# A gated three-branch decoder layer on one core: products moved into two gaps, branch weights told sooner, and work tied behind the ends of projection halves

## The chip, the cores and the metric

The kernel runs on one core of a Trainium2 chip. Its measure is the device time of one execution in microseconds (us), as the median of several runs on the chip. The program is written with a tile framework: Python code issues instructions to the engines, and a scheduler in the framework settles in which order they stand on each engine, within the dependences, by an estimate of its own. A tie (`tc.issue_after(ins)`) asks that what is issued inside it stands behind a given instruction.

## What is computed

One layer over 1024 tokens of width 1024 (cut to what matters here):

```
h = rms_norm(x); parts of h @ w_in go to three branches and their gates
A: sparse attention, 8 heads of 64: an indexer picks 256 keys for each query
B: latent attention, 8 heads, query and key from low-rank projections
M: 4 heads over 256 fixed memory tokens
each branch: (o * silu(z)) @ w_branch, then * sigmoid(gate); the sum @ w_out + x
```

All products run in float32 precision built from two parts: a matrix is split in a high part (suffix h, an FP32R cast on ACT) and a low part (suffix l, the rest, a subtraction on DVE or POOL), and each product is three matmuls, h*h, h*l and l*h (`mm3`, lines 281 to 284).

## The kernel before

**Stages.** In order of time: keys and values of the memory (products `mkps` and `mvps`), the normed and transposed `x` (kept whole as `hTh`, `hTl`), the query of M and its attention, the low-rank projections, attention B from 285 to 511 us, the indexer, branch M (its silu products `z`, `y`, projection `br`) around 690 to 790 us, branch B around 790 to 915 us, the query/key/value projections of A (`qkv(p)` for four pairs of heads: p = 0 runs in the middle of branch M, 1 in the middle of branch B, 2 and 3 behind them), attention A up to about 1220 us, branch A, and the output projection.

**PE's fillers.** The sigmoid gates of all branches are 512-wide products `f` that depend on `hTh` alone. In an attention a `Filler` (lines 360 to 398) hands out such products in steps of one `mm3`: `fill.run(n)` at a place lets n steps out. `PREB` holds four such counts for the start of attention B: at the loading of the first keys, ahead of `k_prep(0, 0)`, ahead of the first `q_prep`, and behind it (lines 560 to 567). `k_prep` transposes the keys `xk` (tile `bkt`), which POOL and DVE have scaled (lines 980 to 983) with a factor that POOL raises to a power (line 238).

**Weights.** `wload` (line 250) issues a DMA into a raw tile, casts it on ACT (line 245) and subtracts on DVE (line 248). Raw tiles have two buffers here (`pool_raw[:] = [2, 8, 768]`), split branch weights seven of 512 columns (`wkind`). Tiles of a kind are handed out in turn, so a load waits until the buffer's last user is done, and what stands behind it in the issuing engine's queue waits too. In `branch` (line 1331) the products go block by block, d = 0 to 7, each in halves j = 0, 1 of 12 matmuls; weights are told up to three blocks, gate values `tg` up to three buffers and attention outputs `osb` two buffers ahead. A half ends in a multiplication on DVE, `ab` for M (line 1400) and `am` for B (line 1408), which frees the PSUM bank, and in a store from POOL's queue.

**The half's remainder.** `qkv(p)` makes 8 tiles of 24 matmuls of 384 columns; each half of four ends in norms and rope on DVE, a power on POOL, and a closure `scaled` (lines 1459 to 1467): the scaling of q on POOL (`a_xq`) and k on DVE (`a_xk`), a cast and subtraction (`a_qs`) and two stores. It is kept in `behind` and run by `catch_up` later: behind the second tile of the next half, ahead of `ab` or `am`, or behind a `z` in `early`. In the tiles' names the pair's half stands first: `a_1xk` is the second half's.

**Background work.** The selection of the 256 keys runs in small steps on ACT and DVE beside all this (names that begin with k, and `idx`).

## Time and profile before

| what | value |
|---|---|
| time, median of 3 runs | 1387.42 us (1385.16 to 1388.04) |
| the profiled execution's own time, and its span | 1386.62 us, 1384.8 us |
| mean granted clock of TensorE, as a share of full speed | 0.995 |
| PE busy, matmuls | 1348.4 us, 97% of the span, 7408 |
| DVE, ACT, POOL busy | 1004.3 us (73%), 708.9 us (51%), 235.0 us (17%) |

Busy time is the time in which an engine had an instruction in work; PE's is drawn from start to modelled end, so consecutive matmuls overlap, and the pace is read from the distance of starts. An idle time carries in brackets the instruction that ended it. Line numbers are those of the kernel before; the changed kernel's lie 7 to 28 lines further down.

### The profile page before, as it was taken

How to read it: one execution, taken by the hardware profiler on the slowest of the kernel's cores; microseconds unless marked ns; L12 is line 12 of the kernel's file. 1: busy time of each engine (PE TensorE's matmuls, PEld its weight loads, DVE VectorE, ACT ScalarE, POOL GpSimd, SP SyncE). 2: the span in 40 equal slices, each digit the busy share in tenths (PEclk: the TensorE clock that was granted, in tenths of full speed). 3: DMA queues.
4: the chain of work that ended last, by engine and by line, in shares of the span. 5: the costliest groups of instructions: out<-in, count | busy, mean ns of one | idle time of the engine just before them, and what ended most of it. 6: DMA issues, size and time to landing. Idle time of an engine off the chain costs nothing. (4 is left out here: it accounts for less than half of the span.)

```text
span 1384.8 us, 20968 instructions
## 1 busy us (share of the span) xinstructions
PE 1348.4 (97%) x7408; PEld 1161.1 (84%) x7408; DVE 1004.3 (73%) x2417; ACT 708.9 (51%) x1546; POOL 235.0 (17%) x271
## 2 busy tenths in 40 slices
PE   8999999999999999999999999999899999999998
PEld 6998888878888888977798889779888888887787
DVE  5945445678888884298787788678858888867883
ACT  6635443256666662164665656543336665653440
POOL 2141002611110101100004201422240000002422
PEclk9999999999999999999999999999999999999999
DMA  7411222231111117310332841792643514218677
GB/s 265 128 47 54 79 63 61 97 88 54 58 43 43 50 32 268 121 54 24 118 103 88 293 108 45 194 208 82 166 154 95 152 55 114 69 61 268 212 202 177
DMA packets 160265, 159.00 MB, mean 115 GB/s; under 512 B 38688, under 2 KB 115488, under 8 KB 160160
## 3 DMA queue, kind: packets, MB, share of 16 engines
q1 hardware_dynamic: 147952, 126.72, 30.4%
q0 software_dynamic: 10592, 28.84, 7.7%
q10 hardware_dynamic: 1616, 2.10, 0.4%
q8 instruction: 58, 0.95, 0.3%
q14 instruction: 47, 0.39, 0.1%
HBM read 106.77 MB, written 50.86 MB: 114 GB/s over the span
## 5 line engine op out<-in xcount | busy, mean ns | idle before, releaser
L1080 ACT ACTIVATE kag<-idx,kaT 128x896 bf16<-128x896 f32 (+2 forms) x96 | 83.2, 866 | 43.5 <-DVE kaT L1101 34.2
L1074 DVE TENSOR_SCALAR_CACHE_REDUCE kdj<-idx,kdT 128x1024 bf16<-128x1024 f32 (+2 forms) x96 | 92.5, 964 | 1.1
L282 PE MATMUL f<-hTh,f_0h 128*128 128x512 f32 x184 | 79.0, 430 | 1.6 <-ACT fo L382 0.9
L282 PE MATMUL f<-hTh,f_1h 128*128 128x512 f32 x184 | 76.1, 414 | 0.0
L283 PE MATMUL f<-hTl,f_1h 128*128 128x512 f32 x184 | 74.2, 403 | 0.0
L284 PE MATMUL f<-hTh,f_1l 128*128 128x512 f32 x184 | 73.9, 402 | 0.0
L284 PE MATMUL f<-hTh,f_0l 128*128 128x512 f32 x184 | 73.8, 401 | 0.0
L283 PE MATMUL f<-hTl,f_0h 128*128 128x512 f32 x184 | 73.5, 399 | 0.0
L1671 POOL TENSOR_TENSOR ac<-ac,tg 128x512 f32<-128x512 f32 x16 | 25.5, 1602 | 253.4 <-DVE tg L1670 250.7
L382 ACT ACTIVATE fo<-f 128x512 f32<-128x512 f32 x48 | 28.8, 601 | 39.7 <-PE f L284 35.9
L1274 ACT ACTIVATE irl<-is 128x512 f32<-128x512 f32 (+1 forms) x80 | 37.7, 527 | 15.4 <-DVE idx L1280 12.6
L282 PEld LDWEIGHTS f<-hTh,f_0h 128*128 128x128 f32 x184 | 35.1, 191 | 8.2 <-ACT fo L382 2.4
L1280 DVE SCALAR_TENSOR_TENSOR idx<-irl,wi,idx 128x1024 f32<-128x1024 f32 (+5 forms) x42 | 39.8, 948 | 1.9 <-ACT irl L1274 0.3
L284 PEld LDWEIGHTS f<-hTh,f_0l 128*128 128x128 f32 x184 | 34.9, 190 | 6.8
L284 PEld LDWEIGHTS f<-hTh,f_1l 128*128 128x128 f32 x184 | 34.7, 188 | 6.0
L283 PEld LDWEIGHTS f<-hTl,f_1h 128*128 128x128 f32 x184 | 34.8, 189 | 4.3
L283 PEld LDWEIGHTS f<-hTl,f_0h 128*128 128x128 f32 x184 | 35.1, 191 | 3.6
L282 PEld LDWEIGHTS f<-hTh,f_1h 128*128 128x128 f32 x184 | 34.7, 189 | 4.1
L1272 PE MATMUL is<-kih,iqT 128*128 128x512 f32 (+1 forms) x80 | 29.7, 376 | 2.3 <-ACT irl L1274 2.1
L237 POOL TENSOR_SCALAR kf<-kss 128x8 f32<-128x8 f32 x8 | 2.3, 285 | 151.7 <-DVE kss L972 146.3
L1273 PE MATMUL is<-kil,iqT 128*128 128x512 f32 (+1 forms) x80 | 27.4, 354 | 0.0
L1317 DVE SCALAR_TENSOR_TENSOR sz<-sz,z 128x512 f32<-128x512 f32 x24 | 16.4, 685 | 14.5 <-ACT sz L1316 14.4
(1331 smaller groups left out, 4825.1 us busy)
## 6 DMA issues: line engine op xcount, KB each, us to landing
s_tg<-fo SPq DMA_DIRECT2D x48, 256.0 KB, 2.0
tg<-s_tg SPq DMA_DIRECT2D x48, 256.0 KB, 4.5
f_0r<-in_w_in_dram SPq DMA_DIRECT2D x23, 256.0 KB, 3.0
f_1r<-in_w_in_dram SPq DMA_DIRECT2D x23, 256.0 KB, 3.0
xx<-in_x_dram SPq DMA_DIRECT2D x8, 512.0 KB, 8.5
tb<-in_w_out_dram SPq DMA_DIRECT2D x16, 256.0 KB, 5.8
s_t<-tb POOLq DMA_DIRECT2D x16, 256.0 KB, 4.7
osb<-s_o SPq DMA_DIRECT2D x16, 256.0 KB, 3.2
```

The source lines that it names most:

```text
L282: nc.tensor.matmul(ps, ah, bh, start=start, stop=False)
L283: nc.tensor.matmul(ps, ah, bl, start=False, stop=False)
L284: nc.tensor.matmul(ps, al, bh, start=False, stop=stop)
L382: nc.scalar.activation(o, ps, AF.Tanh, scale=0.5)
L1074: nc.vector.tensor_scalar(out=junk, in0=idx[t], scalar1=T[:, i:i + 1], scalar2=0.0, op0=ALU.is_ge, op1=ALU.add, accum_out=cnt[:, i:i + 1])
L1080: nc.scalar.activation(junk, idx[t], AF.Sign, bias=T[:, i:i + 1], accum_out=cnt[:, i:i + 1])
L1272: nc.tensor.matmul(sp[:, 0:w], q_, kih[:, k0:k0 + w], start=True, stop=False)
L1273: nc.tensor.matmul(sp[:, 0:w], q_, kil[:, k0:k0 + w], start=False, stop=True)
L1274: nc.scalar.activation(rl[:, k0:k0 + m], sp[:, 0:m], AF.Relu)
L1280: i_ = nc.vector.scalar_tensor_tensor(out=acc[:, 0:n], in0=rl[:, 0:n], scalar=wc, in1=acc[:, 0:n], op0=ALU.mult, op1=ALU.add)
L1317: zi[0] = nc.vector.scalar_tensor_tensor(out=sz, in0=sz, scalar=1.0, in1=pz[j], op0=ALU.add, op1=ALU.mult)
L1671: nc.gpsimd.tensor_tensor(ac, ac, tg, op=ALU.add)
```

## The change

It does six things. (1) The 16 transposes that PE does before its first data come go into one PSUM tile, and 14 more such transposes are tied behind those of the memory's third column block. (2) `PREB` goes from (0, 0, 0, 16) to (0, 12, 0, 7), and `k_prep(0, 0)` is tied behind the last matmul so issued. (3) Weights of branches M and B are told four blocks ahead, with eight buffers; `osb` shares one ring of four buffers with `tg` there. (4) `catch_up` comes behind `ab` or `am` and is tied to it; in `qkv` it is tied behind the copies of the third tile, in `early` behind the `z`. (5) The weights of `qkv(3)` are told inside `early(1, 2)`, ahead of its `z` products. (6) The first tile of `qkv(3)` runs its 16 matmuls with high weights first, and then the 8 with low weights.

```diff
-PREB = (0, 0, 0, 16)
+PREB = (0, 12, 0, 7)
+NWU2 = 14
...
-    for i in range(NWU):
-        nc.tensor.transpose(ps_t(f"wu{i}")[:, 0:P], ident, ident)
+    idle = ps_f("idle")
+    def idle_products(n):
+        for _ in range(n):
+            nc.tensor.transpose(idle[:, 0:P], ident, ident)
+    idle_products(NWU)
...
-        nc.tensor.matmul(ps, al, bh, start=False, stop=stop)
+        last_mm[0] = nc.tensor.matmul(ps, al, bh, start=False, stop=stop)
...
+            if k == 2 and nm == "m":
+                with tc.issue_after(i_.ins):
+                    idle_products(NWU2)
...
         fill.run(pre[1])
-        k_prep(0, 0)
+        with tc.issue_after(last_mm[0].ins) if pre[1] else ExitStack():
+            k_prep(0, 0)
...
-                    wkind[:] = [("wz", 7, 512)] * 2
+                    wkind[:] = [("wz", 8, 512)] * 2
...
-                osb = wk.tile([P, 512], F32, tag="osb", name=f"osb{n}_{w}_{j}", bufs=ob)
+                osb = (wk.tile([P, 512], F32, tag="osb", name=f"osb{n}_{w}_{j}", bufs=ob) if n == 0 else
+                       wk.tile([P, 512], F32, tag="tg", name=f"osb{n}_{w}_{j}", bufs=tgb))
...
-            while len(wb) < min(worder.index(d) + 3, NK):
+            while len(wb) < min(worder.index(d) + (4 if n else 3), NK):
...
-        def catch_up():
-            while behind:
-                behind.pop()()
+        def catch_up(after):
+            with tc.issue_after(after.ins):
+                while behind:
+                    behind.pop()()
...
         def emit_b(d, j, tg, pb):
             ac = t2k(f"ab{d}_{j}")
-            if j:
-                catch_up()
             i_ = nc.vector.scalar_tensor_tensor(out=ac, in0=tg, scalar=1.0, in1=pb, op0=ALU.add, op1=ALU.mult)
+            if j:
+                catch_up(i_)
...
-        def qkv(p):
+        def a_weights(p):
...
+            return pieces, last_load[0]
+        def qkv(p, loaded=None):
+            pieces, last = loaded or a_weights(p)
...
+                    if tb == 0 and p == 3:
+                        for kt in range(NK):
+                            for i_, a_ in enumerate(h_lhs(kt, tb)):
+                                nc.tensor.matmul(ps, a_, pieces[kt // 2][0][:, kt % 2, :],
+                                                 start=kt == 0 and i_ == 0, stop=False)
+                        for kt in range(NK):
+                            nc.tensor.matmul(ps, h_lhs(kt, tb)[0], pieces[kt // 2][1][:, kt % 2, :], start=False,
+                                             stop=kt == NK - 1)
...
-                    if i == 1:
-                        catch_up()
+                    if i == 2:
+                        catch_up(i_)
...
-        def early(a, b):
+        def early(a, b, loaded=None):
             for w in range(a, b):
-                z_early(0, w, C_ZA, wpool, wk, run_topk)
-                catch_up()
-        branch(2, C_ZM, wpool, wk, yp, s_om, emit_b, run_topk, ob=2, mid=lambda: qkv(0))
-        branch(1, C_ZB, wpool, wk, yp, s_o[1], emit_m, run_topk, ob=2, mid=lambda: qkv(1))
+                z_early(0, w, C_ZA, wpool, wk, run_topk, loaded)
+                catch_up(zi[0])
+        branch(2, C_ZM, wpool, wk, yp, s_om, emit_b, run_topk, 4, mid=lambda: qkv(0))
+        branch(1, C_ZB, wpool, wk, yp, s_o[1], emit_m, run_topk, 4, mid=lambda: qkv(1))
...
-        early(1, 2)
-        a3 = qkv(3)
+        a3w = []
+        early(1, 2, lambda: a3w.extend(a_weights(3)))
+        a3 = qkv(3, a3w)
```

Three places show what that does to the order on the engines. A name's ending number is a tile's. First DVE around the last weights of `qkv(3)`, `a3w3l`, at the end of the second half of `qkv(2)` (`a_1`, rope `ar_1`); before:

```order
L441 TENSOR_TENSOR ar_1_1rp_10678<-a_1xq,cos_a 128x64
L442 TENSOR_TENSOR ar_1_1rp_10679<-a_1xq,sin_a 128x64
L1317 SCALAR_TENSOR_TENSOR sz_1_0_10755<-sz_1_0_10755,z_1_0_10705 128x512
L443 TENSOR_TENSOR a_1xq<-ar_1_1rp_10676,ar_1_1rp_10677 128x8x8
L444 TENSOR_TENSOR a_1xq<-ar_1_1rp_10678,ar_1_1rp_10679 128x8x8
L1145 SCALAR_TENSOR_TENSOR kae_10573<-kak_10574,kac,kae_10573 128x896
L1462 TENSOR_TENSOR a_1xk<-a_1xk,a_1rr 128x512
L1147 TENSOR_TENSOR kae_10573<-kae_10573,kas_10568 128x896
L1465 TENSOR_TENSOR a_1qs<-a_1xq,a_1qs 128x8x64
L1149 TENSOR_SCALAR idx_6308<-kae_10573 128x896
L248 TENSOR_TENSOR a3w3l<-a3w3r,a3w3h 128x768
```

and in the changed kernel:

```order
L453 TENSOR_TENSOR ar_1_1rp_10677<-a_1xq,cos_a 128x64
L454 TENSOR_TENSOR ar_1_1rp_10678<-a_1xq,sin_a 128x64
L255 TENSOR_TENSOR a3w3l<-a3w3r,a3w3h 128x768
L455 TENSOR_TENSOR a_1xq<-ar_1_1rp_10675,ar_1_1rp_10676 128x8x8
L456 TENSOR_TENSOR a_1xq<-ar_1_1rp_10677,ar_1_1rp_10678 128x8x8
L1330 SCALAR_TENSOR_TENSOR sz_1_0_10786<-sz_1_0_10786,z_1_0_10736 128x512
L1158 SCALAR_TENSOR_TENSOR kae_10572<-kak_10573,kac,kae_10572 128x896
L1160 TENSOR_TENSOR kae_10572<-kae_10572,kas_10567 128x896
```

`a3w3l` now stands behind the rope's four products, and ahead of the rest of the rope, `sz`, the selection (`kae`, `idx`) and both operations of `scaled` (`a_1xk`, `a_1qs`), which come 13 and 15 rows behind it.

Second, PE at the start of attention B, where the last products of the keys (`kv_7`) end and the first keys are transposed; before:

```order
L284 MATMUL kv_7_3050<-ukv0h,ckvl_1996 128x256
L998 MATMUL bkt_0_3078<-ident,xk_2949 96x128 x4
L282 MATMUL f_5_1_3139<-hTh_1_167,f_5_0h 128x512
L283 MATMUL f_5_1_3139<-hTl_1_183,f_5_0h 128x512
L284 MATMUL f_5_1_3139<-hTh_1_167,f_5_0l 128x512
```

and in the changed kernel:

```order
L291 MATMUL kv_7_3049<-ukv0h,ckvl_1995 128x256
L289 MATMUL f_5_1_3113<-hTh_1_152,f_5_0h 128x512
L290 MATMUL f_5_1_3113<-hTl_1_168,f_5_0h 128x512
L291 MATMUL f_5_1_3113<-hTh_1_152,f_5_0l 128x512
L289 MATMUL f_5_1_3113<-hTh_1_154,f_5_0h 128x512
L290 MATMUL f_5_1_3113<-hTl_1_170,f_5_0h 128x512
L291 MATMUL f_5_1_3113<-hTh_1_154,f_5_0l 128x512
L289 MATMUL f_5_1_3113<-hTh_1_156,f_5_0h 128x512
L290 MATMUL f_5_1_3113<-hTl_1_172,f_5_0h 128x512
L291 MATMUL f_5_1_3113<-hTh_1_156,f_5_0l 128x512
L1011 MATMUL bkt_0_3130<-ident,xk_2948 96x128 x4
L289 MATMUL f_5_1_3113<-hTh_1_158,f_5_1h 128x512
```

Nine gate products stand ahead of `bkt_0` instead of behind it. Between `bkt_0` and `bkt_1` there are now six such products (before, 15), and six more up to the first scores in both; nine of the next gate job stand among the first unit's score matmuls.

Third, DVE in the sixth to seventh block of branch B (`am_0` and `am_1` with `tg_d_j`), with the weights of the following `z` (`z0w`) and of `qkv(2)` (`a2w`); before:

```order
L248 TENSOR_TENSOR z0w_0l<-z0w_0r,z0w_0h 128x512
L1408 SCALAR_TENSOR_TENSOR am_1_10096<-tg_5_1_10081,br_5_1_10083 128x512
L1408 SCALAR_TENSOR_TENSOR am_0_10114<-tg_6_0_10099,br_6_0_10101 128x512
L1099 TENSOR_TENSOR kac<-kac,kan 128x3
L1074 TENSOR_SCALAR kdj_10126,kdc<-idx_6307,kdT 128x768
L1100 TENSOR_SCALAR kar<-kac 128x3
L1101 SCALAR_TENSOR_TENSOR kaT<-kar,kaT 128x3
L248 TENSOR_TENSOR z0w_4l<-z0w_4r,z0w_4h 128x512
L1408 SCALAR_TENSOR_TENSOR am_1_10143<-tg_6_1_10128,br_6_1_10130 128x512
```

and in the changed kernel:

```order
L1421 SCALAR_TENSOR_TENSOR am_1_10095<-tg_5_1_10080,br_5_1_10082 128x512
L255 TENSOR_TENSOR a2w0l<-a2w0r,a2w0h 128x768
L255 TENSOR_TENSOR z0w_4l<-z0w_4r,z0w_4h 128x512
L1421 SCALAR_TENSOR_TENSOR am_0_10113<-tg_6_0_10098,br_6_0_10100 128x512
L1112 TENSOR_TENSOR kac<-kac,kan 128x3
L1087 TENSOR_SCALAR kdj_10125,kdc<-idx_6306,kdT 128x768
L1113 TENSOR_SCALAR kar<-kac 128x3
L1114 SCALAR_TENSOR_TENSOR kaT<-kar,kaT 128x3
L1421 SCALAR_TENSOR_TENSOR am_1_10142<-tg_6_1_10127,br_6_1_10129 128x512
```

The subtractions of `a2w0` and of `z0w_4` have moved ahead of `am_0` of the seventh block, `z0w_0` (not in these rows) to behind the fifth. At the start of the program PE has the 14 transposes, and then six transposes of the memory that stood among the first `mkps` products, ahead of the first `mkps`; all twelve of the first `x0tp` stand ahead of the first `mvps`, of which three stood behind its first two.

## Rows read from the trace of the kernel before

**Rows 1.** The page, busy time (share of the span) and number of instructions of each engine.
```profile
PE 1348.4 (97%) x7408; PEld 1161.1 (84%) x7408; DVE 1004.3 (73%) x2417; ACT 708.9 (51%) x1546; POOL 235.0 (17%) x271
```

**Rows 2.** What PE waited for: us in total, times, longest us.
```profile
PE a L283 <- DVE a3w3l L248: 4.5, 1, 4.5
PE mkps L282 <- ACT mTh L352: 2.6, 1, 2.6
PE bkt L998 <- POOL xk L983: 2.5, 1, 2.5
...
PE z L282 <- DVE am L1408: 1.6, 1, 1.6
...
PE br L282 <- DVE am L1408: 1.4, 1, 1.4
PE br L282 <- DVE ab L1400: 1.1, 1, 1.1
...
PE a L283 <- DVE a2w3l L248: 0.9, 1, 0.9
```

**Rows 3.** Stretches of 10 us: busy time by engine, PE's clock, DMA share, GB/s.
```profile
890.00:900.00 10.00, 8.61 (x38) 6.62 (x37) 5.23 (x13) 4.59 (x10) 1.72 (x2) 1.00 1.10 277
980.00:990.00 10.00, 8.97 (x36) 8.97 (x37) 8.60 (x17) 3.54 (x9) 1.09 (x2) 0.66 0.78 248
```

**Rows 4.** PE's timeline, last projection: start, us, instruction, [idle before <- releaser].
```profile
973.01 0.34 PE L282 MATMUL a<-a3w0h,hTh 128*128 128x384 f32 x1
...
976.17 0.33 PE L282 MATMUL a<-a3w3h,hTh 128*128 128x384 f32 x1
981.03 0.69 PE L283 MATMUL a<-a3w3l,hTh 128*128 128x384 f32 x1 [4.53 <-DVE a3w3l L248]
...
986.63 0.43 PE L282 MATMUL a<-a3w2h,hTh 128*128 128x384 f32 x1
```

**Rows 5.** DVE's timeline, same place.
```profile
977.04 1.62 DVE L1462 TENSOR_TENSOR a_1xk<-a_1xk,a_1rr 128x512 f32<-128x512 f32 x1
...
980.02 0.95 DVE L248 TENSOR_TENSOR a3w3l<-a3w3r,a3w3h 128x768 fp32r<-128x768 f32 x1
```

**Rows 6.** ACT's timeline, same place.
```profile
973.73 0.84 ACT L245 CAST a3w3h<-a3w3r 128x768 fp32r<-128x768 f32 x1 [2.28 <-DMA a3w3r<-in_w_in_dram]
```

**Rows 7.** PE's timeline, start of attention B.
```profile
287.36 1.09 PE L998 MATMUL bkt<-ident,xk 128*96 128x128 f32 x4 [2.47 <-POOL xk L983]
...
292.78 0.60 PE L998 MATMUL bkt<-ident,xk 128*96 128x128 f32 x4
...
294.82 0.40 PE L1028 MATMUL b_3S<-bkh,b_3qh 96*128 96x512 f32 x1
```

**Rows 8.** POOL's and DVE's timelines, same place.
```profile
286.17 1.14 POOL L983 TENSOR_TENSOR xk<-kro,kf 128x256 f32<-128x256 f32 x1
...
287.68 1.64 POOL L238 TENSOR_TENSOR kf<-kf,mhalf 128x8 f32<-128x8 f32 x1
...
290.49 0.42 DVE L983 TENSOR_TENSOR xk<-kro,kf 128x256 f32<-128x256 f32 x1
```

**Rows 9.** DVE's timeline, branch M, third block of products.
```profile
756.40 0.69 DVE L1462 TENSOR_TENSOR a_1xk<-a_1xk,a_1rr 128x512 f32<-128x512 f32 x1 [0.51 <-POOL a_1rr L238]
```

**Rows 10.** ACT's and DVE's timelines, branch B, sixth block of products.
```profile
896.64 0.62 ACT L245 CAST b1w6h<-b1w6r 128x512 fp32r<-128x512 f32 x1 [4.65 <-DMA b1w6r<-in_w_branch_dram]
...
898.02 0.16 DVE L1099 TENSOR_TENSOR kac<-kac,kan 128x3 f32<-128x3 f32 x1 [4.45 <-ACT kag L1080]
```

**Rows 11.** DVE's timeline, last products of branch B.
```profile
912.34 0.69 DVE L1408 SCALAR_TENSOR_TENSOR am<-tg,br 128x512 f32<-128x512 f32 x1 [2.77 <-DMA tg<-s_tg]
```

**Rows 12.** PE's and ACT's timelines, start of the program.
```profile
27.80 1.22 PE L282 MATMUL mvps<-hTh,mTh 128*128 128x512 f32 x2 [1.39 <-ACT hTh L245]
28.82 0.84 PE L350 MATMUL x0tp<-ident,xx 128*128 128x128 f32 x3
...
27.12 1.14 ACT L245 CAST hTh<-mvw 128x512 fp32r<-128x512 f32 x2 [2.38 <-DMA mvw<-in_w_mem_kv_dram]
```

More of the change, by code (lines that the diff above doesn't have):

```diff
@@ L283, in mm3 @@
         nc.tensor.matmul(ps, ah, bl, start=False, stop=False)
-        nc.tensor.matmul(ps, al, bh, start=False, stop=stop)
+        last_mm[0] = nc.tensor.matmul(ps, al, bh, start=False, stop=stop)
+    last_mm = [None]
     def proj_w(nm, pool, w, cols, nk, per=None, held={}):
@@ L349, in norm_T @@
             for i, xt in enumerate(xs):
-                nc.tensor.transpose(tp[:, i * P:(i + 1) * P], xt[:, k * P:(k + 1) * P], ident)
+                i_ = nc.tensor.transpose(tp[:, i * P:(i + 1) * P], xt[:, k * P:(k + 1) * P], ident)
+            if k == 2 and nm == "m":
+                with tc.issue_after(i_.ins):
+                    idle_products(NWU2)
             hi, lo = dst(k)
@@ L1397, in emit_b @@
             ac = t2k(f"ab{d}_{j}")
+            i_ = nc.vector.scalar_tensor_tensor(out=ac, in0=tg, scalar=1.0, in1=pb, op0=ALU.add, op1=ALU.mult)
             if j:
-                catch_up()
-            i_ = nc.vector.scalar_tensor_tensor(out=ac, in0=tg, scalar=1.0, in1=pb, op0=ALU.add, op1=ALU.mult)
+                catch_up(i_)
             nc.gpsimd.dma_start(acc_at(d, j), ac)
@@ L1405, in emit_m @@
             ac = t2k(f"am{d}_{j}")
+            i_ = nc.vector.scalar_tensor_tensor(out=ac, in0=tg, scalar=1.0, in1=pb, op0=ALU.add, op1=ALU.mult)
             if j:
-                catch_up()
-            i_ = nc.vector.scalar_tensor_tensor(out=ac, in0=tg, scalar=1.0, in1=pb, op0=ALU.add, op1=ALU.mult)
+                catch_up(i_)
             nc.gpsimd.dma_start(acc_at(d, j), ac, accum_op=ALU.add)
             run_topk(i_, 2.6)
-        def qkv(p):
+        def a_weights(p):
             c = P * p
@@ L1420, in qkv @@
             ws[:] = WSG
-            last = last_load[0]
+            return pieces, last_load[0]
+        def qkv(p, loaded=None):
+            pieces, last = loaded or a_weights(p)
             for j in range(2):
@@ L1433, in qkv @@
                     ps = ps_turn(f"a{p}_{tb}", GAB)[:, 0:384]
-                    for kt in range(NK):
-                        ah, al = h_lhs(kt, tb)
-                        wh, wl = pieces[kt // 2]
-                        mm3(ps, ah, al, wh[:, kt % 2, :], wl[:, kt % 2, :], kt == 0, kt == NK - 1)
+                    if tb == 0 and p == 3:
[6 more added lines that the diff above has]
+                                             stop=kt == NK - 1)
+                    else:
+                        for kt in range(NK):
+                            ah, al = h_lhs(kt, tb)
+                            wh, wl = pieces[kt // 2]
+                            mm3(ps, ah, al, wh[:, kt % 2, :], wl[:, kt % 2, :], kt == 0, kt == NK - 1)
                     psv = ps.rearrange("p (e h d) -> p e h d", e=3, h=2)
@@ L1441, in qkv @@
                     run_topk(i_, 4.2)
-                    if i == 1:
-                        catch_up()
+                    if i == 2:
+                        catch_up(i_)
                 for e, x_ in enumerate((xk, xq)):
@@ L1487, in hybrid_kernel @@
         ws[:] = WSG
-        def early(a, b):
+        def early(a, b, loaded=None):
             for w in range(a, b):
-                z_early(0, w, C_ZA, wpool, wk, run_topk)
-                catch_up()
-        branch(2, C_ZM, wpool, wk, yp, s_om, emit_b, run_topk, ob=2, mid=lambda: qkv(0))
-        branch(1, C_ZB, wpool, wk, yp, s_o[1], emit_m, run_topk, ob=2, mid=lambda: qkv(1))
+                z_early(0, w, C_ZA, wpool, wk, run_topk, loaded)
+                catch_up(zi[0])
+        branch(2, C_ZM, wpool, wk, yp, s_om, emit_b, run_topk, 4, mid=lambda: qkv(0))
+        branch(1, C_ZB, wpool, wk, yp, s_o[1], emit_m, run_topk, 4, mid=lambda: qkv(1))
         early(0, 1)
```

## The prediction

> **What bounds the kernel now.** The page's busy times come first: PE works 1348.4 of the span's 1384.8 us, DVE 1004.3, ACT 708.9 [rows 1]. No other engine is near the span, so the end is set by PE, and a change that leaves PE's products alone can take away only PE's 36.4 us without work and what a lower clock costs it. The second view lists what PE waited for [rows 2]: seven waits that the change touches make 4.5 + 2.6 + 2.5 + 1.6 + 1.4 + 1.1 + 0.9 = 14.6 us, and each happens once. The third view is the table by stretches [rows 3]: in 890 to 900 us PE stands idle for 1.39 us and its granted clock stays 1.00, the 2.4 GHz level; in 980 to 990, behind an idle 4.53 us, it is 0.66 on average, part of the stretch at 1.2 GHz. So a wait of about 1.5 us costs itself, a long one costs itself and a slow stretch behind it. The reader is to see in the timelines what ends each wait, and whether the change moves that.
>
> The sum is made against the profiled execution's own 1386.62 us; the runs' median, 1387.42, lies 0.8 above, and the time that I give is the median less the gain.
>
> **The last projection, `qkv(3)`.** PE starts at 973.01, runs 18 matmuls to 976.17 at 3.16 / 18 = 0.176 us each, waits for `a3w3l` until 981.03, and then needs 5.60 us for 17 intervals, 0.329 each, before the pace is back at 986.63 [rows 4]. The wait costs 4.5 us, the slow stretch 17 x (0.329 - 0.176) = 2.6, together 7.1. What is late is not the weight: its cast on ACT ends at 973.73 + 0.84 = 974.57 [rows 6]. The subtraction starts at 980.02 because DVE has `a_1xk` (1.62 us from 977.04) and more in front of it [rows 5], part of `scaled`, which needs POOL. In the new order `a3w3l` stands behind the rope's four products, and all of `scaled` behind it, so it can start at 974.6 and end 0.95 later, 975.6. With the first tile's 16 high products first, PE wants it at the 23rd matmul, 973.01 + 22 x 0.176 = 976.9. The wait goes with 1.3 us to spare, and the slow stretch with it: I take 7.0, at most 7.1. The raw tiles of the last two weights still come free no earlier than before, so telling them sooner moves nothing there; if their DMA, for which ACT waits 2.28 us [rows 6], comes 2 us later against a PE that is ahead, 0.7 us of wait remain, and with a slow stretch some 4 us of gain: the lower end. Late next is `scaled`; it feeds stores that attention A reads later.
>
> **The start of attention B.** PE waits 2.47 us for the keys' first half, until 287.36 [rows 7], and POOL ends that at 286.17 + 1.14 = 287.31 [rows 8], which no edit moves. From there to the second keys `bkt_1` at 292.78 PE does `bkt_0` and 15 gate products in 5.42 us. Nine of the 15 now stand ahead of `bkt_0`, inside the wait. What is left takes at most 0.74 + 6/15 of the rest, some 2.7 us, and would let `bkt_1` start at 290.0; but the second half of the keys then ends the wait: POOL's power ends at 287.68 + 1.64 = 289.32, and DVE's two multiplications ended at 290.49 + 0.42 = 290.91 [rows 8]. Between 289.32 + 1 and 290.91, `bkt_1` starts 1.9 to 2.4 us sooner, and the six products up to the scores at 294.82 [rows 7] with it. I take 2.1, at whichever clock. Ends: 1.0 (nine gate products now stand among the first scores, whose DVE and ACT work they can hold up) and 2.5. The number of gate products stays; they are only taken earlier.
>
> **Branch M.** The wait of 1.1 us for `ab` comes from DVE: `a_1xk` stood ahead of `ab` and waited until 756.40 for POOL's power [rows 9]. It now stands behind `ab`. I take 1.1, between 0 and 1.1.
>
> **Branch B.** ACT's cast of `b1w6` waited 4.65 us for its DMA, the selection's `kag` stood behind it, DVE's `kac` waited 4.45 for that, and `am` behind `kac` cost PE 1.4 [rows 2, 10]. That weight is now told a block sooner; 24 matmuls of 512 columns take 24 x 0.176 x 512 / 384 = 5.6 us as an estimate from rows 4, more than the 4.65. I take 1.3 of 1.4. The 1.6 us of `z` [rows 2] go back to `am` waiting 2.77 us for its `tg` [rows 11]; with a ring of four instead of three the load goes out half a block, 2.8 us, sooner. I take 1.3 of 1.6. `a2w3l` now stands ahead of the selection's long operations: 0.7 of 0.9. All three end at 0 below, for the new order also puts `a2w0l` and `z0w_4l` ahead of the seventh block's `am` on DVE, and both hang on DMAs.
>
> **The start.** The 14 transposes fill a wait of 2.6 us that ends with ACT, and six transposes of the memory go ahead of the first product. What comes of it is absorbed: before `mvps` PE waits 1.39 us for a cast at 27.12 which waited 2.38 for the DMA of `mvw` [rows 12], and that DMA waits for nothing on PE. Only the three `x0tp` (0.84 us at 28.82) that now stand ahead of `mvps` can go into the wait. I take 0.4, between 0 and 0.8.
>
> **Sum:** 7.0 + 2.1 + 1.1 + 1.3 + 1.3 + 0.7 + 0.4 = 13.9 us. The profiled execution would be 1386.62 - 13.9 = 1372.7, the median 1387.42 - 13.9 = **1373.5 us**. The ends add up to 7.1 + 2.5 + 1.1 + 1.4 + 1.6 + 0.9 + 0.8 = 15.4 (1372.0) and 4 + 1.0 = 5.0 (1382.4).
>
> **Rivals.**
> 1. *The DMA engines are the limit in branch B.* In 890 to 900 us their share is 1.10 [rows 3], that is full: a load told sooner may only push another one back, and the three gains there (1.3 + 1.3 + 0.7) stay away: 13.9 - 3.3 = 10.6, 1376.8 us. Against it: the ring of four and the deeper weights move loads into the block before, and PE's waits there were single ones. The Trainium skill, "DMA: Bandwidth & Descriptors", section "Issuing engines are not separate DMA queues", says that all transfers run on the same 16 DMA engines and interleave, whoever starts them; by that rule the gain of branch B is 0 and the time 1376.8. The trace agrees as to the share, and does not show whether earlier stretches have room enough. Chance 0.14.
> 2. *`a3w3l` is still late.* Its DMA, or the rope ahead of it, comes 2 us or more after PE wants it, and the clock falls again: 2 us of wait and 2.6 us of slow pace remain, 13.9 - 4.6 = 9.3, 1378.1 us. For it: ACT did wait for that DMA [rows 6]; against it: 1.3 us to spare. Chance 0.10.
> 3. *The start gains too.* If PE's products of the memory run at full clock from the first, and the transposes and norms of `x` behind them come sooner, up to the whole wait of 2.6 us is won instead of 0.4: 1371.3 us. Against it stands the wait for `mvw` [rows 12]. Chance 0.08. The other way round, that the idle transposes do nothing, costs 0.4 us and lies within the forecast.
> 4. *Slower: ACT's casts become the bound in the branches.* The weights of the block three ahead take buffers that PE frees with the last matmul of the block before, and on ACT the selection's `kag` stands behind the cast, as it did behind `b1w6h` [rows 10]. Four blocks of each branch are loaded that way, 8 casts. Without the branches' own 1.3 + 1.3 the gain is 11.3; 0.2% slower begins when each cast costs PE (11.3 + 2.8) / 8 = 1.8 us, more than the one of rows 10 did (1.4). At 2.9, midway to the 4.45 of that row, 8 x 2.9 - 11.3 = 11.9 more: 1399.3 us. Against it: seven buffers had the same wait for the subtraction. Chance 0.04.
> 5. *The gains are given back*, several of the above at once, or the new order of the first unit of attention B holds up DVE: 1385 to 1389 us. Chance 0.06.
>
> **How the numbers follow.** The forecast has 0.58. A measurement of this kernel tells about 0.2% from no change, 2.8 us, so faster means below 1384.6. The forecast and rivals 1 to 3 lie there, 0.90, less 0.01 for their upper ends: 0.89. Rival 5 gives 0.07 for no change, rival 4 gives 0.04 for slower. The range holds the forecast's ends and rivals 1 to 3, and leaves out 4 and 5: 1369.5 (a start that gains, on top of the upper ends, less what the runs scatter) to 1382.5 (the lower ends).
>
> **What would show it.** In the changed profile: no wait of PE for `a3w3l`, a clock of 1.00 behind it and 16 of the first matmuls in one run; `bkt_0` still at POOL's `xk`, less than 1 us of idle before it and another short wait at `bkt_1`; no wait of `br` for `ab`; in branch B ACT's casts of the last weights without a wait for DMA; the first `mvps` where it was. The forecast is wrong if PE's idle time stays above 26 us, if a wait for `a3w3l`, `am` or `bkt` over 2 us is left, or if new waits appear behind the casts in the branches.

## The result, and the profile after

The changed kernel takes **1377.48 us**, the median of 3 runs (1376.06 to 1378.31), against 1387.42: a ratio of 0.9933, with a 95% interval from 0.9918 to 0.9948. That is 9.9 us less, where the prediction summed 13.9 and gave 1373.5 in a range from 1369.5 to 1382.5. The profiled execution of the changed kernel took 1376.06 us, 10.56 less than that of before.

The busy times of the page, to be held against [rows 1]:

```profile
span 1374.3 us, 21012 instructions
PE 1344.6 (98%) x7422; PEld 1158.0 (84%) x7422; DVE 1004.9 (73%) x2417; ACT 708.3 (52%) x1546; POOL 232.7 (17%) x271
```

PE works 3.8 us less and idles 29.7 us (1374.3 - 1344.6) instead of 36.4. So of the 10.5 us by which the span is shorter 6.7 are idle time; the other 3.8 are less time for products of which none was taken away. What PE waits for (operation waited with, engine and operation waited for; us in total, times, longest) answers to [rows 2]:

```profile
PE f L289 <- ACT fo L394: 3.4, 5, 1.3
PE is L1285 <- ACT irl L1287: 3.0, 5, 0.9
PE mtp L359 <- DVE mTl L365: 2.9, 1, 2.9
...
PE z L289 <- DVE am L1421: 1.2, 1, 1.2
PE bkt L1011 <- DVE xk L996: 1.1, 1, 1.1
...
PE qmps L289 <- ACT qmw2h L252: 0.6, 1, 0.6
...
PE bkt L1011 <- POOL xk L996: 0.4, 1, 0.4
```

The waits for `a3w3l`, `ab`, `a2w3l` and the `am` of `br` are gone. That for `bkt` went from 2.5 to 1.1 + 0.4. `z` still waits 1.2 for `am`. At the start 2.9 for `mtp` stand where 2.6 for `mkps` stood, and 0.6 for `qmps` are new. `f` waits 3.4 instead of 0.9 for `fo`, the tanh on ACT that takes a gate product's result out of PSUM, and `is`, the indexer's scores, 3.0 instead of 2.1 for ACT. The stretches of [rows 3] (us, then busy time and instructions of PE, PEld, DVE, ACT, POOL, then granted clock, DMA share, GB/s):

```profile
890.00:900.00 10.00, 10.00 (x45) 8.04 (x44) 7.43 (x20) 4.28 (x10) 3.56 (x5) 1.00 1.08 230
910.00:920.00 10.00, 8.79 (x39) 6.83 (x38) 6.86 (x14) 4.72 (x9) 1.73 (x2) 1.00 0.93 191
980.00:990.00 10.00, 10.00 (x58) 10.00 (x58) 9.57 (x22) 4.55 (x12) 0.24 (x1) 1.00 0.37 111
```

At 980 to 990 PE is now busy all the time at 1.00, which is the 2.4 GHz level, where it was 0.66. The last projection's PE timeline (start, length, engine, line, operation, tiles), against [rows 4]:

```profile
970.34 0.34 PE L1456 MATMUL a<-a3w0h,hTh 128*128 128x384 f32 x1
...
972.97 0.34 PE L1456 MATMUL a<-a3w3h,hTl 128*128 128x384 f32 x1
973.15 0.51 PE L1459 MATMUL a<-a3w0l,hTh 128*128 128x384 f32 x2
...
974.21 0.51 PE L1459 MATMUL a<-a3w3l,hTh 128*128 128x384 f32 x2
```

Sixteen high products come first, the eight low ones at 973.15, and `a3w3l` at 974.21 follows with no gap, at the pace of 0.176 us throughout. DVE's timeline there, against [rows 5]:

```profile
968.36 0.96 DVE L255 TENSOR_TENSOR a3w3l<-a3w3r,a3w3h 128x768 fp32r<-128x768 f32 x1 [0.91 <-ACT a3w3h L252]
...
976.98 0.67 DVE L1490 TENSOR_TENSOR a_1xk<-a_1xk,a_1rr 128x512 f32<-128x512 f32 x1
...
978.50 0.68 DVE L1493 TENSOR_TENSOR a_1qs<-a_1xq,a_1qs 128x512 fp32r<-128x512 f32 x1
```

and ACT's, against [rows 6]:

```profile
967.49 0.83 ACT L252 CAST a3w3h<-a3w3r 128x768 fp32r<-128x768 f32 x1 [1.84 <-DMA a3w3r<-in_w_in_dram]
...
970.81 0.62 ACT L1492 CAST a_1qs<-a_1xq 128x512 fp32r<-128x512 f32 x1 [1.99 <-POOL a_1xq L1490]
```

`a3w3l` starts as soon as its cast ends, and both operations of `scaled` come 8 to 10 us after it. ACT's `a_1qs` also has to wait for POOL, 1.99 us, but PE waits for nothing that stands behind it.

The balance, from the starts of PE instructions in the two profiled executions (later by the change: minus):

| from, to | won in the stretch | predicted |
|---|---|---|
| span's start to `bkt` (287.36, now 288.50) | -1.1 | +0.4 |
| `bkt` to the first `br` (742.72, now 744.57) | -0.7 | +2.1 |
| first `br` to attention A's first scores `a_3S` (1031.94, now 1022.29) | +11.5 | +11.4 |
| `a_3S` to the end | +0.9 | 0 |

The four add up to 10.6. All that was predicted between the branches and attention A came; nothing of what was predicted ahead of them did, and 1.8 us more were lost.

The other three lines are differences of single executions, and small ones. Over all the traces of this document, from `a_3S` to the end of the span takes 351.7 to 354.8 us, so the +0.9 says nothing. The two lines ahead of the branches are set against the other traces below. The third is clear of such scatter: 289.2 us before, 277.7 in the change.

### The profile page after: what moved, and what is told of

Same layout as the page of the kernel before. It is cut to its first block, busy times and chain, and to the rows that moved or that the text cites. A ratio compares the mean times of both kernels' runs of the same rounds, so it can differ in the third digit from the quotient of the medians.

```text
span 1374.3 us, 21012 instructions
## 1 busy us (share of the span) xinstructions
PE 1344.6 (98%) x7422; PEld 1158.0 (84%) x7422; DVE 1004.9 (73%) x2417; ACT 708.3 (52%) x1546; POOL 232.7 (17%) x271
## 5 line engine op out<-in xcount | busy, mean ns | idle before, releaser
L289 PEld LDWEIGHTS f<-hTh,f_0h 128*128 128x128 f32 x184 | 34.7, 188 | 11.3 <-ACT fo L394 6.0
```

What stands on the lines that cost most here:

```text
L289: nc.tensor.matmul(ps, ah, bh, start=start, stop=False)
```

## The experiments

Each kernel was run beside the kernel before on the same chip (medians of before: 1387.23 us beside e1 to e4, 1388.12 beside e5 to e8, 1389.18 beside e9 to e12), so the ratios are to be compared, not the medians; a ratio need not be the quotient of two medians. A ratio's interval is some 0.0015 to either side, so two variants are told apart from about 3 us on.

| label | what it is | median us | ratio to before, 95% interval |
|---|---|---|---|
| e1_qkv3_alone | before, with edits (5) and (6) | 1386.66 | 0.9998 [0.9986, 1.001] |
| e5_no_ties | the change without (4) | 1386.02 | 0.9986 [0.9973, 0.9998] |
| e9_ties_alone | before, with (4) | 1378.41 | 0.9923 [0.9908, 0.9939] |
| e12_no_emit_ties | the change; (4) only in `qkv` and `early` | 1379.81 | 0.9935 [0.992, 0.995] |
| e7_no_hi_first | the change without (6) | 1377.53 | 0.9922 [0.9906, 0.9939] |
| e8_told_late | the change without (5) | 1377.21 | 0.9915 [0.99, 0.993] |
| e6_no_branch | the change without (3) | 1382.67 | 0.9956 [0.9941, 0.9971] |
| e10_ties_and_branch | before, with (3) and (4) | 1380.36 | 0.9937 [0.9922, 0.9952] |
| e2_no_start | the change without (1) | 1378.13 | 0.9945 [0.9929, 0.9962] |
| e3_preb_back | the change without (2) | 1376.94 | 0.9932 [0.9917, 0.9946] |
| e4_preb_13 | the change with 16 steps in `PREB` | 1376.37 | 0.9929 [0.9914, 0.9944] |
| e11_best | e4_preb_13 without (1) | 1376.97 | 0.9903 [0.9885, 0.992] |

The theory was that of the prediction: `scaled` out of the way of `a3w3l`, with early telling and the high products first as its helpers, and single waits removed one by one. The rivals: the tie alone does it; the tie is not needed where the weight is told early; what is won early is given back later.

### The last weights alone

```diff
-        early(1, 2)
-        a3 = qkv(3)
+        a3w = []
+        early(1, 2, lambda: a3w.extend(a_weights(3)))
+        a3 = qkv(3, a3w)
...
+                    if tb == 0 and p == 3:
...
```

> The kernel before with two parts of the change alone: the weights of qkv(3) told ahead of the z products, and its first tile with the high products first. Theory of the prediction: the wait for a3w3l (4.5 us) and the slow stretch (2.6 us) go, 7.0 us faster, 1380.4 us. Rival: the deferred scaling (a_1xk, a_1qs) stays ahead of a3w3l on DVE, because its tie is not in this kernel, and the wait stays: 1387.4 us, or 2 to 3 us faster for the six products that come before the weight is wanted.

Measured: 0.9998. PE's waits hold no `a3w3l`, but two that before did not have:

```profile
PE z L284 <- ACT a_1xv L1458: 2.0, 1, 2.0
PE f L284 <- DVE sz L1322: 1.9, 1, 1.9
```

ACT's timeline shows the first of them. Behind the cast of `a_0qs`, which waits for POOL, stand three tiles' copies, nine in all:

```profile
1013.51 0.62 ACT L1482 CAST a_0qs<-a_0xq 128x512 fp32r<-128x512 f32 x1 [7.62 <-POOL a_0xq L1480]
```

The kernel before has the same wait at the same place, and PE did not feel it, for it was some 7 us behind: the `z` products that e1_qkv3_alone is ready for at 1012.66 start there at 1019.67, and the nine copies are done at 1015.47.

```profile
1013.33 0.62 ACT L1464 CAST a_0qs<-a_0xq 128x512 fp32r<-128x512 f32 x1 [7.63 <-POOL a_0xq L1462]
```

In the changed kernel the same cast comes 9 us sooner, with one tile's copies behind it, and no wait of PE follows:

```profile
1004.33 0.62 ACT L1492 CAST a_0qs<-a_0xq 128x512 fp32r<-128x512 f32 x1 [3.63 <-POOL a_0xq L1490]
```

The stretches of e1_qkv3_alone, columns as above:

```profile
980.00:990.00 10.00, 10.00 (x59) 10.00 (x58) 7.39 (x13) 3.38 (x10) 0.79 (x2) 1.00 0.72 232
1010.00:1020.00 10.00, 7.98 (x28) 6.07 (x27) 5.43 (x14) 4.27 (x14) 5.16 (x8) 0.83 0.26 101
1020.00:1030.00 10.00, 8.09 (x32) 6.31 (x32) 4.85 (x14) 2.08 (x4) 7.09 (x11) 0.83 0.43 161
```

So the slow stretch of 980 to 990 is gone, and two of 0.83 stand 30 us later. Attention A's first scores start at 1032.36, before at 1031.94. What follows: with edits (5) and (6) alone the wait for `a3w3l` goes, but `scaled` then holds up other operations that PE waits for, and nothing is won.

### The change without its ties, and the ties alone

```diff
-                    if i == 2:
-                        catch_up(i_)
+                    if i == 1:
+                        catch_up()
...
-                catch_up(zi[0])
+                catch_up()
...
-            if j:
-                catch_up(i_)
```

(the last call stands ahead of `ab` and `am` again, as before, and `catch_up` has no `issue_after`).

> The changed kernel with the deferred scaling as it was: run ahead of ab and am, behind the second tile's copies in qkv, untied. Theory drawn from the kernel with qkv(3)'s two parts alone, which was no faster than before: the tie is what makes the stretch of qkv(3) gain, since without it ACT's cast a_qs, which waits some 7 us for POOL, stands ahead of the tile's copies and PE waits twice 2 us for a bank, with a slow stretch behind each. Then this kernel is 1.1 us (ab) plus some 6 us slower than the changed one, 1384 to 1386 us, with the waits near 1014 and 1024 us and no wait for a3w3l. Rival: ring and depth in the branches, not the tie, keep qkv(3) clear: only the 1.1 us for ab return, 1378.6 us.

Measured: 0.9986, of the change's gain four fifths are lost. PE's waits between 905 and 1040 us:

```profile
PE z L289 <- DVE am L1422: 4.5, 1, 4.5
PE f L289 <- DVE sz L1330: 3.5, 1, 3.5
PE z L289 <- ACT a_1xv L1467: 1.3, 1, 1.3
```

No `a3w3l`, but `sz` and `a_1xv` as in e1_qkv3_alone, and `am` with 4.5: the load of `a2w0r`, whose cast stands ahead of it, went out at 904.29 us instead of 902.87 and was cast at 912.18 instead of 909.02 (the change). Why the load is later there was not followed further. `a_3S` starts at 1031.94, to the hundredth where it started before.

The kernel before with the ties only:

```diff
-        def catch_up():
-            while behind:
-                behind.pop()()
+        def catch_up(after):
+            with tc.issue_after(after.ins):
+                while behind:
+                    behind.pop()()
...
-                    if i == 1:
-                        catch_up()
+                    if i == 2:
+                        catch_up(i_)
...
```

> The kernel before with the ties of the deferred scaling alone. If, as the runs so far suggest, nothing but the ties and the branches' buffers moves the time, this is the changed kernel without the branches' buffers: some 5 us faster than before, 1382.5 us, with no wait for a3w3l although its weights are told as late as before, and with waits of PE left in branch B and for a2w3l. Rival: the wait for a3w3l needs the early telling as well and stays: 1386 us or more.

Measured: 0.9923, as fast as the whole change within the intervals, and 4 us faster than expected. PE's waits between 905 and 1040:

```profile
PE a L285 <- DVE a2w3l L250: 1.3, 1, 1.3
PE z L284 <- DVE am L1412: 0.9, 1, 0.9
```

`a3w3l` is not among them, though it is told as late as before and the products stand in the old order, in which it is wanted at the 20th matmul. DVE has it in time:

```profile
971.73 1.80 DVE L250 TENSOR_TENSOR a3w3l<-a3w3r,a3w3h 128x768 fp32r<-128x768 f32 x1
...
979.71 0.69 DVE L1481 TENSOR_TENSOR a_1xk<-a_1xk,a_1rr 128x512 f32<-128x512 f32 x1
```

and PE takes it at its pace:

```profile
974.37 0.34 PE L285 MATMUL a<-a3w3l,hTh 128*128 128x384 f32 x1
```

1.80 us from 971.73 is 973.53, 0.84 ahead of PE; `a_1xk` of `scaled` comes 6 us after. From the first `br` to `a_3S` this kernel takes 279.0 us, 10.2 less than before, of the 11.5 that the whole change wins there. What follows: edit (4) carries the gain, and the rival that the tie alone does it was right. Edit (4) both asks for `scaled` later in the program (behind the third tile's copies and not the second's) and ties it there; which of the two is needed no run separates. "Ties" stands for both here.

Which of the ties? With those at `ab` and `am` taken back:

```diff
-            if j:
-                catch_up(i_)
...
+            if j:
+                catch_up()
             i_ = nc.vector.scalar_tensor_tensor(out=ac, in0=tg, scalar=1.0, in1=pb, op0=ALU.add, op1=ALU.mult)
```

> The changed kernel with the scaling ahead of ab and am again and untied there, while the ties in qkv and early stay. The kernel without any tie lost 8.5 us: a longer wait of z for am (4.5 us instead of 1.2) and 1.4 + 3.5 us of waits with a slow stretch in and behind qkv(3). If the ties at ab and am carry the first and those in qkv the rest, this kernel loses some 3.5 us, 1381 us, and keeps qkv(3) free of waits. If the waits in qkv(3) come from the order in the branches too, it loses most of the 8.5, 1385 us.

Measured: 0.9935. The ties in `qkv` and `early` are those that count; the ones in the branches are not seen in the time, though `z` there waits 1.88 us for `am` instead of 1.21.

### High products first, and weights told early, each taken away

```diff
-                    if tb == 0 and p == 3:
+                    if False:
```

> The changed kernel with the first tile of qkv(3) in the usual order, high and low weights in turn. The low part of the last weights is then wanted at the 20th matmul, 3.3 us behind the tile's start, instead of the 23rd, 3.9 us. The prediction had 1.3 us to spare with the high products first, so 0.8 us are left without: no wait, and no difference, 1377.5 us. Rival: the high weights of the fourth pair, cast late by ACT, or their low parts hold PE, a wait of 1 us or more and a slow stretch: 1379 to 1381 us.

```diff
-        early(1, 2, lambda: a3w.extend(a_weights(3)))
-        a3 = qkv(3, a3w)
+        early(1, 2)
+        a3 = qkv(3)
```

> The changed kernel with the weights of qkv(3) told in qkv(3), behind the z products, as before. If, as the prediction says, the tie takes the scaling out of a3w3l's way and the raw tiles come free no sooner, telling them late costs nothing: 1377.5 us. Rival: told late, they stand behind the z's evacuation on ACT and DVE and PE waits for a weight of qkv(3), 2 to 7 us: 1379.5 to 1384.5 us.

Measured: 0.9922 and 0.9915, the change has 0.9933; neither has a wait for `a3w3l`. Each is a reserve for a wait that the ties have already removed; e9_ties_alone leaves out both at once, and has no such wait either.

### The branches' weights

```diff
-                    wkind[:] = [("wz", 8, 512)] * 2
+                    wkind[:] = [("wz", 7, 512)] * 2
-            while len(wb) < min(worder.index(d) + (4 if n else 3), NK):
+            while len(wb) < min(worder.index(d) + 3, NK):
...
```

(and `osb` in its own two buffers again).

> The changed kernel with the branches' weights and buffers as they were (three blocks ahead, seven buffers, osb with two buffers of its own, tg three). The prediction's terms: 1.3 (am) + 1.3 (z, of which the changed kernel got 0.4) + 0.7 (a2w3l) come back, 2.4 us slower than the changed one, 1379.9 us, with ACT's cast of b1w6 waiting for its DMA again. Rival 1 of the prediction, the DMA engines are full there anyway: no difference, 1377.5 us.

Measured: 0.9956, 5 us above the change's median. The intervals of these two still touch, but that of e6_no_branch lies clear of e7_no_hi_first's and e8_told_late's, which were run beside it and are as fast as the change. The trace has the place. PE's waits between 905 and 1040, and the stretch behind them:

```profile
PE a L290 <- DVE a2w3l L255: 2.4, 1, 2.4
```

```profile
930.00:940.00 10.00, 9.37 (x39) 9.37 (x40) 8.19 (x19) 2.71 (x10) 1.14 (x2) 0.68 0.57 157
```

`z` no longer waits for `am`, and `qkv(2)` waits for its weights instead, with a slow stretch behind. The other way round, depth added to the ties alone:

```diff
-            while len(wb) < min(worder.index(d) + 3, NK):
+            while len(wb) < min(worder.index(d) + (4 if n else 3), NK):
...
```

> The kernel before with the ties and the branches' weights and buffers, and nothing else of the change: start, start of attention B and qkv(3)'s weights and order are as before. If the other three parts are worth nothing together, it is as fast as the changed kernel, 1376.5 to 1378 us; if they are worth the prediction's 2.1 + 0.4 us and what qkv(3) gains by early weights, 1380 us or more.

Measured: 0.9937, no gain over e9_ties_alone's 0.9923. There `z` waits 2.62 us for `am` and the clock of 910 to 920 is 0.83. And e9_ties_alone, with the old depth too, does not lose what e6_no_branch loses: PE begins `qkv(2)` at 924.51 there and at 923.17 in e6_no_branch, `a2w3l` is ready at 929.28 and at 930.57, so the wait is 1.3 in the one, and 0.2 + 0.8 + 2.4 with a slow stretch in the other. So what the deeper weights are worth hangs on a few us of arrival at this place; a value by itself was not settled, nor why `a2w3l` is ready later in e6_no_branch.

### The start, and attention B

```diff
-    idle_products(NWU)
+    for i in range(NWU):
+        nc.tensor.transpose(ps_t(f"wu{i}")[:, 0:P], ident, ident)
...
-NWU2 = 14
+NWU2 = 0
...
```

> The changed kernel with the start as it was (16 transposes in three rotating tiles, none tied behind the memory's third column block). The prediction had the 14 transposes gain 0.4 us: this kernel would be 0.4 us slower than the changed one, 1377.9 us. What the trace after suggests instead: the changed start loses 1.2 us (the attention on the memory stands 1.2 us later than before), because the memory's next transposes stand ahead of the first mkps and wait 2.9 us for DVE, and this kernel is 1.2 us faster, 1376.3 us, with mkps at 9.3 us again.

Measured: 0.9945, no difference from the change that can be told, but in the trace the last scores of attention M start at 158.91 instead of 160.89, 2.0 us sooner. Of these 1.0 is left at `a_3S` (1021.32) and none at the last product `oT` (1369.98 and 1369.94).

```diff
-PREB = (0, 12, 0, 7)
+PREB = (0, 0, 0, 16)
```

> The changed kernel with the gate products at the start of attention B as they were, 16 behind the first q_prep. The prediction's 2.1 us: this kernel is 2.1 us slower than the changed one, 1379.6 us. What the trace after suggests: the first scores are 2.3 us later again, but the three new waits of a gate product for ACT's tanh (0.48 us each, in attention B) and the late weight cast in the indexer go too, so that it is only 0.5 to 1 us slower, or the same, 1377.5 to 1378.5 us.

```diff
-PREB = (0, 12, 0, 7)
+PREB = (0, 12, 0, 4)
```

> The changed kernel with PREB (0, 12, 0, 4): the gap at the start of attention B is filled as in the change, but 16 gate steps are let out ahead of the first scores, as before the change, and not 19. If the three new waits of 0.48 us for the tanh come from the gate products standing three steps further in their job, they go and this kernel is 1.4 us faster than the changed one, or more with the indexer's part (1.4), 1374.7 to 1376.1 us. If they come from the nine products among the first scores or from the fill of the gap itself, they stay: 1377.5 us.

Measured: 0.9932 and 0.9929. With the old `PREB` the wait of 2.48 us for `bkt` is back and the time is the same. With 16 steps in all, as before, but 12 of them taken early, PE's waits between 290 and 520 us hold a single one longer than 0.3 us, the 1.1 for `bkt`, where the change, with 19 steps, has this one besides:

```profile
PE f L289 <- ACT fo L394: 1.5, 3, 0.5
```

and the first `br` starts at 742.50 instead of 744.57. Yet `a_3S` starts at 1022.18, only 0.11 sooner: `z` then waits 1.89 for `am`, and the clock of 910 to 920 falls to 0.83.

### Both of these together

```diff
-PREB = (0, 12, 0, 7)
+PREB = (0, 12, 0, 4)
-NWU2 = 14
+NWU2 = 0
...
```

> The changed kernel with the start as before and PREB (0, 12, 0, 4). From the traces the start costs the change 1.2 us and the three extra gate steps some 2 us by the end of the indexer; but each of the two runs that undid one of them ended within 1.2 us of the changed kernel, because the branches and the last stage vary by 2 us between runs. If the two add up: 1374.5 to 1375.5 us, the fastest of all. If what is won ahead of the branches is lost in them, where DMAs set the pace: 1376.5 to 1377.5 us.

Measured over 5 rounds: 0.9903, the lowest of all, but its interval reaches 0.992 and that of the change begins at 0.9918, so it is not shown to be faster. Its six runs lie apart, two at 1371.7 and 1372.9 us and four from 1376.4 to 1378.1; the trace is of one of the four. In it PE is 3.7 us ahead at the first `br` (740.84), and 0.3 behind at `a_3S` (1022.60). DVE's timeline at the end of branch B, in the change:

```profile
909.88 0.96 DVE L255 TENSOR_TENSOR a2w0l<-a2w0r,a2w0h 128x768 fp32r<-128x768 f32 x1 [3.16 <-ACT a2w0h L252]
...
913.27 0.69 DVE L1421 SCALAR_TENSOR_TENSOR am<-tg,br 128x512 f32<-128x512 f32 x1
```

and in e11_best:

```profile
907.62 0.96 DVE L250 TENSOR_TENSOR a2w0l<-a2w0r,a2w0h 128x768 fp32r<-128x768 f32 x1 [4.57 <-ACT a2w0h L247]
...
911.01 0.69 DVE L1413 SCALAR_TENSOR_TENSOR am<-tg,br 128x512 f32<-128x512 f32 x1
```

The `am` shown is the one that `z` waits for; one more `am` stands between. `a2w0l` stands ahead of both, and waits for ACT's cast, which in e11_best waits for a load:

```profile
906.75 0.84 ACT L247 CAST a2w0h<-a2w0r 128x768 fp32r<-128x768 f32 x1 [4.26 <-DMA a2w0r<-in_w_in_dram]
```

That load goes out 3.7 us sooner than in the change (899.2 and 902.9), but its cast starts only 2.3 us sooner (906.75 and 909.02). The stretch with the idle 2.94 us:

```profile
910.00:920.00 10.00, 8.16 (x24) 6.51 (x25) 6.27 (x15) 5.19 (x9) 2.60 (x3) 0.66 0.87 189
```

PE starts `z` at 914.10, 912.5, 913.6 and 911.8 in the change, e4_preb_13, e10_ties_and_branch and e11_best; the first `br` of the four lies 3.7 us apart, `a_3S` only 1.1. **In these four the end of branch B takes up most of what was won before it**, as a longer wait and a slower stretch behind it (the waits are 1.21, 1.89, 2.62 and 2.94 us, the clock of 910 to 920 is 1.00, 0.83, 0.83 and 0.66). Putting `am` ahead of `a2w0l`, or the load earlier, was not tried.

## Why the prediction was right, point by point

The time lies in the range and the largest term came where and as large as it was forecast; of the rest three terms failed, and the sum was 4.0 us too high.

**The last projection, 7.0: right in place and size, in mechanism half of it, and too generous to two helpers.** From the first product of `qkv(3)` to `a_3S` PE takes 51.95 us instead of 58.93, which is 7.0 less. The wait and the slow stretch went, with `scaled` behind `a3w3l`. The prediction put part of it down to the high products first, with "1.3 us to spare"; e7_no_hi_first and e8_told_late show that neither they nor the early telling was needed, and e9_ties_alone that the ties suffice.

The step that failed here, to the forecast's advantage, is that the raw tiles "come free no earlier than before". The ties brought the weight too. ACT before, where the casts of the first two weights stand behind six copies and `a_0qs`, the first half's `scaled`, which waits for POOL:

```profile
959.61 0.62 ACT L1464 CAST a_0qs<-a_0xq 128x512 fp32r<-128x512 f32 x1 [7.68 <-POOL a_0xq L1462]
...
962.01 0.88 ACT L245 CAST a3w0h<-a3w0r 128x768 fp32r<-128x768 f32 x1
```

and in the changed kernel, where those copies stand ahead of it:

```profile
956.60 0.62 ACT L1492 CAST a_0qs<-a_0xq 128x512 fp32r<-128x512 f32 x1 [0.88 <-POOL a_0xq L1490]
957.12 0.83 ACT L252 CAST a3w0h<-a3w0r 128x768 fp32r<-128x768 f32 x1
```

With these casts and their subtractions the raw tiles come free, so the load of `a3w3r` went out at 962.13 instead of 967.78. `a3w3l` was done at 969.32, 4.9 us ahead of PE, and not 1.3. e9_ties_alone, which tells the weight late, has that load at 963.07, and e1_qkv3_alone, which tells it early without the ties, at 967.43: it is the ties that moved it. That the helpers were not needed fits this; whether they would have been without it no run shows.

The prediction also called `scaled` harmless when late ("it feeds stores that attention A reads later"): true where it is tied. Untied, it holds up the copies and `sz` of `qkv(3)` itself, a wait that the kernel before hides (7.63 us of ACT at 1013.33), which the prediction did not list and which cost e1_qkv3_alone all it had won.

**Branch M, 1.1 and branch B, 1.3 + 0.7: the waits went** (1.14, 1.39 and 0.88 in the traces), but the causes named are not shown to be the ones. For `ab` the prediction named the tie: e12_no_emit_ties, with the deeper weights and no tie there, has no such wait either, while e1_qkv3_alone, with neither, waits 1.7 us; so either of the two suffices. For `br`'s `am` it named the weight told a block sooner: ACT's casts of the last weights do not wait for a DMA any more, but e9_ties_alone, where the cast of `b1w6` still waits 4.83 us and `kac` 4.46, has no wait of `br` either, and e6_no_branch one of 0.4. For `a2w3l` it named the order on DVE: with the old depth PE waits 1.3 in e9_ties_alone and 2.4 in e6_no_branch, with the deeper weights in no trace, and the load of `a2w3r` goes out at 916.66 in the change, at 920.52 in e9_ties_alone and at 923.11 before.

**`z`, 1.3: mis-sized, it was 0.4** (1.59 to 1.21). The step that failed is the choice of the upper end: the wait for `tg` went, and what the prediction named as the lower end took its place, `a2w0l` and `z0w_4l` ahead of the seventh block's `am`, waiting for a load. Nor did the ring and the depth gain anything for `z`: it waits 1.2 to 2.9 us in each run that has them and the ties in `qkv`, and 0.95 and 0 in e9_ties_alone and e6_no_branch, which have not. The DMA share is 1.08 at 890 to 900, as full as before, and 1.11 at 900 to 910, where this load is under way (before 1.02). The Trainium skill, "DMA: Bandwidth & Descriptors", section "Issuing engines are not separate DMA queues", has all transfers run on the same 16 DMA engines and interleave. The trace agrees as to the share. Rival 1, that the branch's gains therefore stay away, came true for `z` alone: the two other waits went.

**Attention B, 2.1: right at its place, wrong at the end.** PE's timeline, against [rows 7]:

```profile
288.50 0.64 PE L1011 MATMUL bkt<-ident,xk 128*96 128x128 f32 x4 [0.41 <-POOL xk L996]
...
291.65 0.62 PE L1011 MATMUL bkt<-ident,xk 128*96 128x128 f32 x4 [1.11 <-DVE xk L996]
...
293.72 0.40 PE L1041 MATMUL b_3S<-bkh,b_3qh 96*128 96x512 f32 x1
```

`bkt` waits 0.41 and 1.11, as foreseen, and from the first `bkt` to the scores `b_3S` PE takes 5.22 us instead of 7.46, so 2.2 were won. (Two roundings of the prediction are a tenth off there: what is left takes 0.74 + 6/15 of 4.68 = 2.6 us, and 292.78 - 290.32 is 2.5; the 2.1 does not hang on them.) The step that failed is "the number of gate products stays": 19 steps instead of 16 are taken, and three waits of 0.48 for `fo` appeared, which e4_preb_13 removes. They are 1.5 of the 2.8 us by which the stretch up to `br` misses. The other 1.3 lie within the scatter: from `bkt` to the first `br` the five traces with the old `PREB` take 455.1 to 457.2 us, 456.0 on average, the seven with the change's 455.3 to 456.7, 455.8 on average, and the two with 16 steps (e4_preb_13, e11_best) 454.2. So some 1.8 us of the forecast 2.1 can be had there, and the change as it stands has about 0.2 of them. Rival 5, gains given back, is what happened here, in the size of one term.

**The start, 0.4: wrong in sign, -1.1.** The step that failed is "what comes of it is absorbed". PE's timeline:

```profile
5.71 1.69 PE L150 MATMUL idle<-ident 128*128 128x128 f32 x14
10.27 1.22 PE L359 MATMUL mtp<-ident,mx 128*128 128x128 f32 x6 [2.87 <-DVE mTl L365]
11.25 0.48 PE L289 MATMUL mkps<-mkw0h,mTh 128*128 128x512 f32 x1
...
11.91 0.63 PE L291 MATMUL mkps<-mkw0h,mTl 128*128 128x512 f32 x1
...
14.95 0.45 PE L290 MATMUL mkps<-mkw1l,mTh 128*128 128x512 f32 x1
```

and DVE's operation that ends the wait:

```profile
9.74 1.26 DVE L365 SCALAR_TENSOR_TENSOR mTl<-mtp,gm_c,mTh 128x256 fp32r<-128x256 f32 x3
```

The fourteen idle transposes take 1.69 us and not the wait's length: they take 0.12 us each, where the 16 at the very start take 0.22 (3.58 in all). Then the six transposes of the memory, moved ahead of the first product, wait until 10.27 for DVE, so that `mkps` starts at 11.25 instead of 9.26. From 11.91 to 14.95 consecutive products start 0.43 us apart, and 0.23 behind it. `mvps` starts 0.6 sooner, at 27.20, but its last product, at 43.29, 0.4 later than before, and 0.64 more is waited for `qmw2h`. The prediction bounded this term at 0 below, though no reason excluded a loss. The size is uncertain, since the start of the first `bkt` scatters: from 285.75 to 288.40 in the six traces with the old start (287.0 on average), from 288.07 to 288.70 in the eight with the new one (288.5). The sign holds in these averages, 1.4 us; in the runs' times, e2_no_start against the change, no difference can be told.

**Its own sign.** It said that the forecast is wrong if PE's idle time stays above 26 us. It is 29.7, so by this sign it was wrong, though the time lies in the range. The sum implied 36.4 - 11.3 = 25.1 (2.6 of the 13.9 are slow pace, not idle time); of the 4.6 above it `fo` makes 2.5, `is` 0.9 and `z` 0.9. The other signs came out: no wait for `a3w3l` and a clock of 1.00 behind it, 0.41 and 1.11 at the two `bkt`, no wait of `br` for `ab`, and ACT's casts of branch B's last weights without a wait for DMA; the first `mvps` came 0.6 us sooner than it was.

## What to carry to other kernels

A deferred chain that waits for a slow engine holds up whatever stands behind it on the others, here ACT for 7.6 to 7.7 us twice, with copies and weight casts behind: put its tail behind the operations that PE waits for next, before buying buffers and earlier loads for them. Here that alone was worth, within the intervals, what all six edits were. An edit that removes a wait should be asked which wait stands hidden behind it, and where the next wait for a load is: here most of what was won ahead of branch B's end was taken up there. And a filling product is to be sized by what it takes in the trace, not by the gap: here 14 of them filled 1.69 of 2.6 us, and the next thing put behind them waited longer than the first had.

## What the runs showed of the hardware

Idle times of PE and the mean clock of the 10 us around their end, as rows of these runs have them: 1.21 us at 914 left the stretch of 910 to 920 at 1.00 (1.59 before did too), 1.89 and 2.62 went with 0.83, 2.94 with 0.66, and behind 4.48 in e5_no_ties 918 to 920 has 0.50. It is no plain rule: in e5_no_ties 3.45 us at 1025 left 1020 to 1030 and 1030 to 1040 at 1.00, and the products behind it start 0.23 us apart. At the start of the kernel before, the granted clock of 8 to 14 us reads 1.00 while equal products start 0.43 us apart, against 0.23 from 14.1 on; so there the pace has to be read from the timeline, not from the clock's column (e2_no_start, with the same start, has the 0.43 and reads 0.50).
